# Attention values stored as high beside low: two products a step instead of three

## The chip, the cores and the metric

The kernel runs on one core of one Trainium2 chip, in one launch. The metric is the device time of a launch in microseconds (us). A core has a matrix engine (PE in the profile; PEld is its loading of the stationary operand), a vector engine (DVE), a scalar engine (ACT), a general engine (POOL), and a queue that issues transfers (SP). Each engine takes its own instructions strictly in the order in which they were written for it, and waits where an input or a buffer is not ready. Matrix products land in eight banks (PSUM) of 128 partitions by 512 float32 numbers; everything else lies in SBUF.

## The reference, cut to what matters

A small encoder: two layers on 512 tokens of width 1024, each of feed-forward block, token mixer, cross-attention into 256 memory tokens, and feed-forward block. The change is in the token mixer of the even layer, which runs once:

```python
def mixer_ab(h, w_in, w_out, q_gain, k_gain, sink, ang_2d, ang_1d):
    qa, ka, va, qb, kb, vb = jnp.split(h @ w_in, AB_SPLITS, axis=-1)
    ...
    out_a = global_gqa(qa, ka, va)              # 8 heads of 64, 2 key/value heads, all 512 keys
    ...
    out_b = window_gqa_sink(qb, kb, vb, sink)   # 8 heads of 64, keys within 128 tokens, a sink logit
    return jnp.concatenate([out_a, out_b], axis=-1) @ w_out
```

Each head computes softmax(q k) v. All is float32, and the kernel has to stay close to float32: it splits every operand z into a high part zh, rounded to the matrix engine's fast float32 form, and a low part zl = z - zh, and adds several products of the parts.

## The kernel before, in words

**Parts and products.** `split` (line 296) makes the parts of a tile with two instructions: ACT casts the source to the high part, DVE subtracts that from the source. `mm3` (line 307) then adds three products: high by high, high by low, low by high. A product of a stationary 128 by 128 tile and a moving tile of up to 512 columns is one MATMUL with one LDWEIGHTS.

**The even mixer** (`mixer_ab`, line 709) projects the tokens into queries, keys and values (lines 797 to 811), and then goes through 16 heads, numbered n: 0 to 7 are the dense A heads, 8 to 15 the windowed B heads. Two heads s = 0 and 1 make a pair that fills 128 rows of output, 64 each. The loop stands at lines 917 to 937. For each head it

- turns the softmax weights of this head (`turned`, line 857): for each block kk of 128 keys up to four PE transposes into a bank of kind "t", then a split into two parts in SBUF;
- computes the softmax weights of the head two further on (`weights_a`, line 819, or `weights_b`, line 834): scores on PE into banks of kind "a", a minimum over the keys on DVE, an exponential on ACT, a reciprocal on DVE, and a multiplication that POOL does for most blocks (`normalise`, line 648);
- multiplies the turned weights with the values (`attend`, line 867) into a bank of kind "d";
- does a piece of other work laid aside for this place: the last 512 columns of the projection (`last_columns`, A heads), or a quarter of a half of the output projection (`share`, B heads), both on PE into "d" banks as well.

An A head has 512 columns in each of four key blocks; a B head has 256, 384, 384 and 256, since a block of keys is seen by two or three blocks of queries.

**Values before.** `padded` (line 703) takes two slabs (SBUF tiles of 4 KB a partition, 27 in all), one for high and one for low, and clears them on POOL. In them a value head of 64 columns stands in a stationary tile of 128 columns beside 64 columns of zeros: on the left for s = 0, on the right for s = 1. So both heads of a pair add into one bank, each into its own 64 rows. `attend` calls `mm3`, three products for each key block, 24 for a pair. At the end of a pair the bank is split straight out of PSUM: one cast on ACT, one subtraction on DVE (lines 926 and 930).

**What sets the order.** All operations are first recorded (class `Graph`, line 64) with their tiles. `emit` (line 168) then goes through them with costs of its own for each instruction and writes each engine's instructions in the order in which they come ready by these costs, older ones first. Tiles of a kind are granted in the order in which they were asked for: 27 slabs, 14 smaller tiles "t2", 2 raw weight buffers, and banks "a" 3, "d" 2, "t" 3. A bank is granted anew when the last instruction that uses it has ended. So a change of a few instructions also moves others on every engine of this stage, since the planner places them anew.

**After the heads** the other half of the output projection follows (`down`, lines 938 to 940). Its weights come through the two raw buffers, of which one is held by the memory tokens until they are turned (`memory_tokens`, after head 13).

The odd layer's mixer (`mixer_c`, line 955) holds its values in another way: high and low side by side, two products for each block of weights, and at lines 1087 to 1092 a copy and an addition that bring the two halves together.

Of the kernel before, what the change touches and what calls it, by code (L numbers as in the profile page):

```python
# [12 lines left out]
F32 = mybir.dt.float32  # L13
F32R = mybir.dt.float32r
# [3 lines left out]
ALU = mybir.AluOpType  # L18
AX = mybir.AxisListType

P = 128
D = 1024
S = 512
NT = S // P
# [4 lines left out]
ROWS = S // GRID_W  # L29
# [223 lines left out]
class Kernel:  # L253
# [446 lines left out]
        )  # L700
        return sq[:, :w]

    def padded(self):
        tiles = [self.slab(F32R, (P, NT, 2, P)) for _ in range(2)]
        for z in tiles:
            self.nc.gpsimd.memset(z.bitcast(F32), 0.0)
        return tiles

    def mixer_ab(self, ln_i, last):
        nc, a = self.nc, self.a  # L710
        w_in, w_out = a["ab_w_in"], a["ab_w_out"]
# [3 lines left out]
        def halves():  # L715

            if not room:
                z = self.slab(F32, (P, 2, 512))
                room.extend([z[:, 0, :], z[:, 1, :]])
            return room.pop(0)  # L720
# [3 lines left out]
        for name, gain in (("q", "ab_q_gain"), ("k", "ab_k_gain"), ("b", None)):  # L724
            tab = halves()
            tab = tab.rearrange("p (t d) -> p t d", t=NT)
            src = a["rope_1d"] if gain is None else a["rope_2d"]
            for t in range(NT):
                nc.sync.dma_start(out=tab[:, t, :], in_=src.rearrange("(r c) d -> c r d", c=GRID_W)[16 * t : 16 * t + 16])
            if gain:  # L730
                gn = self.small(128, "gain", 1)
                nc.sync.dma_start(out=gn[:, 0:64], in_=a[gain][0:1, :].broadcast_to([P, 64]))
                for h in range(2):
                    nc.sync.dma_start(
                        out=gn[:, 64 + 32 * h : 96 + 32 * h],
# [18 lines left out]
            v = z.rearrange("p (pr s d) -> p s pr d", s=2, d=64)  # L754
            return v if s is None else v[:, s]

        def value(src, vp, t, n=1):

            dst = []
            for z in vp:  # L760
                v = z[:, t].rearrange("p v c -> p (v c)")
                dst.append(bass.AP(v.tensor, v.offset, [list(v.ap[0]), [256, n], [192, 2], [1, 64]]))
            self.split(src.rearrange("p (t v c) -> p t v c", t=n, v=2), *dst)

        def by_rows(z, natural):

# [19 lines left out]
        def keys(tile_, natural):  # L786

            got = []
            for s in range(2):
                ps = self.transposed([(t * P, P, tile_[:, t, s].rearrange("p c d -> p (c d)")) for t in range(NT)])  # L790
                both = self.pair()
                shape = lambda y: y.rearrange("p (r c) -> p r c", r=ROWS) if natural else y
                self.split(by_rows(ps, natural), *(shape(z) for z in both))
                got.append(both)
            return got

        w1, w0 = self.w_cols512(w_in, 512), self.w_cols512(w_in, 0)
        qa, qb, va = [halves() for _ in range(NT)], [halves() for _ in range(NT)], self.padded()
        ka, kb = (self.slab(F32, (P, NT, 2, 2, 64)) for _ in range(2))
        q = [self.pair()]  # L800
        for cg, t in ((1, 0), (1, 1), (1, 2), (0, 0), (1, 3), (0, 1), (0, 2), (0, 3)):
            ps = proj(self.ps("a"), t, w1 if cg else w0)
            if cg == 0:
                self.rope(self.rms(ps, 8), 8, tabs["q"], t, pairs(qa[t]))
                queries(qa, 0, False, q[0], [t])
                continue
            self.rope(self.rms(ps[:, 0:128], 2), 2, tabs["k"], t, ka[:, t])
            value(ps[:, 128:256], va, t)
            self.rope(ps[:, 256:512], 4, tabs["b"], t, pairs(qb[t], 0))
            if t == NT - 1:  # L810
                kA = keys(ka, False)
# [45 lines left out]
        def turned(p):  # L857

            got = []
            for kk in range(NT):  # L860
                ts = [t for t in range(NT) if (t, kk) in p]
                pt = self.transposed([(t * P, P, p[t, kk]) for t in ts])
                lo, hi = ts[0] * P, (ts[-1] + 1) * P
                got.append((lo, hi, [z[:, lo:hi] for z in self.split_t2(pt, lo, hi)]))
            return got

        def attend(po, s, pts, vp):
            for kk, (lo, hi, pt) in enumerate(pts):
                v = [z[:, kk, s, :] for z in vp]
                self.mm3(po[:, lo:hi], v, pt, s == 0 and kk == 0, s == 1 and kk == NT - 1, skip_group_check=True)  # L870

        w2 = self.w_cols512(w_in, 1024)
        vt, vt_, qb_ = self.t2(F32), [], {}
# [11 lines left out]
        def values_turned():  # L887
            ps = self.transposed([(t * P, P, vt[:, t * P : (t + 1) * P]) for t in range(NT)])
            vt_.append(self.t2(F32))
            nc.scalar.copy(vt_[0].rearrange("p (r c) -> p r c", r=ROWS), by_rows(ps, True))  # L890

        def values_b():
            value(self.transposed([(t * P, P, vt_[0][:, t * P : (t + 1) * P]) for t in range(NT)]), vb, 0, NT)

        def share(h, t):
            self.down_bank(acts[:4], [[z[:, b] for z in wa[h][b0]] for b0 in range(2) for b in range(2)], t, h, 1.0 / ALPHA)
# [4 lines left out]
        aside = {}  # L901
        for n in range(8):
            aside.setdefault((-1, -1, -1, 0, 1, 2, 3, 4)[n], []).append(lambda n=n: last_columns(n // 2, n % 2))
        vb, kB, wa, acts = [], [], {}, []
        aside.setdefault(2, []).append(lambda: vb.extend(self.padded()))
        aside.setdefault(5, []).append(lambda: (values_turned(), kB.extend(keys(kb, True))))
        aside[6] = [values_b]
        for n in range(8):
            h, t = divmod(n, 4)
            if t == 0:  # L910
                aside.setdefault(6 + 4 * h, []).append(lambda h=h: half_rows(h))
            aside.setdefault(8 + n, []).append(lambda h=h, t=t: share(h, t))
        heads = [(f, v, pr, s) for f, v in ((weights_a, va), (weights_b, vb)) for pr in range(4) for s in range(2)]
        us, po = [g(*at) for g, _, *at in heads[:2]], None
        for g in aside[-1]:
            g()
        for n, (f, v, pr, s) in enumerate(heads):
            pts = turned(us.pop(0))
            for g, _, *at in heads[n + 2 : n + 3]:
                us.append(g(*at))  # L920
            if s == 0:
                po = self.ps("d")
            attend(po, s, pts, v)
            if s == 1:
                if n < 8:
                    acts.append(self.split_t2(po))
                else:

                    h, l = self.pair()
                    self.split(  # L930
                        po.rearrange("p (r c) -> p c r", r=ROWS), *(z.rearrange("p (c r) -> p c r", r=ROWS) for z in (h, l))
                    )
                    acts.append((h, l))
            for g in aside.get(n, []):
                g()
            if n == 13:
                self.memory_tokens()
# [400 lines left out]
```

## Time and profile before

| | |
|---|---|
| time, median of 3 runs | 2215.97 us (2215.14 to 2216.75) |
| span of the profiled execution | 2218.7 us, 2.7 us above that median; no other time of this execution is given |
| PE busy | 2185.8 us, 99% of the span, 11264 products |
| PEld / DVE / ACT / POOL busy | 84% / 64% / 40% / 14% |
| the chain that ended last | PE 94%, DVE 3%, ACT 1%, POOL 1%, DMA 1%, issue 1% |
| mean granted PE clock | 0.996 |
| the even mixer in the span | from about 352 to about 584 us |

Shares are taken over the whole span, which strings together stages with different limits. A matrix product's own duration in the trace (382 ns on average) overlaps the next one's, so the pace is read from long stretches of products in the chain. "Idle before" is the time an engine stood still ahead of an instruction, with the one that released it. Nearly all instructions are recorded by a helper at line 143, so groups are told apart by the names of their tiles: "a", "d" and "t" are banks, but "t" is also the name that the "t2" tiles get, since numbers are left out.

### The profile page before, as it was taken

Reading aid. Unit: us, or ns where it says so; the run is one execution under the profiler, and the core shown is the slowest. Engines: PE = TensorE matmul, PEld = TensorE weight load, DVE = VectorE, ACT = ScalarE, POOL = GpSimd, SP = SyncE. Lnnn points to the kernel's source line nnn. Section 1 sums busy time; section 2 is a strip of 40 time slices with the busy share of each in tenths; the row PEclk is TensorE's granted clock in tenths of the full one; section 3 lists DMA queues with packets and bytes.
Section 4 is the critical chain, followed back from the end, with each engine's and each line's share of the span. In section 5 each row is a group of like instructions: output and inputs, shape, how many; then the busy total and the mean of one; then the engine's idle time right before and its main releaser. Section 6 shows DMA issues by size and latency. Waiting matters only on the chain.

```text
span 2218.7 us, 28479 instructions
## 1 busy us (share of the span) xinstructions
PE 2185.8 (99%) x11264; PEld 1863.8 (84%) x11264; DVE 1415.7 (64%) x2127; ACT 878.2 (40%) x1412; POOL 318.0 (14%) x431
## 2 busy tenths in 40 slices
PE   8999999999999999999999999999999999999998
PEld 7888888778998988888888888888989989888886
DVE  5566657788745756655765566567767557566556
ACT  4333333466443433333333233245554434333331
POOL 0000022544000000000300001214330000000002
PEclk9999999999999999999999999999999999999999
DMA  7443333102442642334334444235553325433342
GB/s 222 143 142 120 106 107 104 39 10 70 130 133 96 182 135 95 95 121 149 120 105 131 143 142 147 95 102 148 141 157 124 124 96 161 124 100 93 111 152 67
DMA packets 195221, 265.15 MB, mean 120 GB/s; under 512 B 8848, under 2 KB 139536, under 8 KB 195088
## 3 DMA queue, kind: packets, MB, share of 16 engines
q1 hardware_dynamic: 181136, 231.88, 32.9%
q0 software_dynamic: 13952, 31.46, 6.6%
q8 instruction: 88, 1.44, 0.3%
q14 instruction: 45, 0.37, 0.1%
HBM read 248.63 MB, written 4.19 MB: 114 GB/s over the span
## 4 chain that ended last, share of the span: by engine, by line
PE 94%; DVE 3%; ACT 1%; POOL 1%; DMA 1%; issue 1%; SPq 0%; DVEq 0%; POOLq 0%; ACTq 0%
PE a L143 59%; PE d L143 21%; PE t L143 14%; DVE slab L143 1%; DVE t L143 1%; ACT slab L143 1%; DVE x L143 0%; POOL slab L143 0%; DMA raw<-ab_w_out 0%; ACT t L143 0%; DMA slab<-t 0%; POOL rms8y L143 0%; ACT junk L143 0%; DMA x<-x 0%; POOL lny L143 0%
## 5 line engine op out<-in xcount | busy, mean ns | idle before, releaser
L143 PE MATMUL a<-xh,slab 128*128 128x512 f32 (+1 forms) x2960 | 892.9, 382 | 0.0
L143 PEld LDWEIGHTS a<-xh,slab 128*128 128x128 f32 x2960 | 549.1, 188 | 106.8
L143 PE MATMUL a<-xl,slab 128*128 128x512 f32 (+1 forms) x1480 | 565.1, 382 | 0.0
L143 PE MATMUL d<-slab,slab 128*128 128x512 f32 (+2 forms) x1856 | 448.8, 381 | 3.3 <-ACT slab L143 3.3
L143 DVE TENSOR_TENSOR slab<-raw,slab 128x1024 fp32r<-128x1024 f32 x300 | 368.8, 1250 | 92.7 <-ACT slab L143 92.2
L143 PEld LDWEIGHTS d<-slab,slab 128*128 128x128 f32 x1856 | 334.5, 188 | 67.3 <-ACT slab L143 5.1
L143 ACT CAST slab<-raw 128x1024 fp32r<-128x1024 f32 x300 | 304.3, 1048 | 206.2 <-DMA raw<-ffn_w_gate 176.4
L143 DVE TENSOR_TENSOR slab<-slab,slab 128x1024 fp32r<-128x1024 f32 (+2 forms) x220 | 254.0, 1177 | 177.8 <-ACT slab L143 104.7
L143 PEld LDWEIGHTS a<-xl,slab 128*128 128x128 f32 x1480 | 278.3, 188 | 53.4
L143 PE MATMUL a<-slab,slab 128*128 128x256 f32 (+3 forms) x1720 | 301.2, 321 | 3.7 <-DMA slab<-t 1.4
L143 PEld LDWEIGHTS a<-slab,slab 128*128 128x128 f32 x1720 | 250.0, 190 | 31.4 <-DVE slab L143 4.6
L143 ACT ACTIVATE t<-a 128x512 f32<-128x512 f32 (+3 forms) x105 | 58.1, 554 | 525.7 <-PE a L143 525.6
L143 ACT CAST slab<-slab 128x1024 fp32r<-128x1024 f32 (+1 forms) x180 | 174.3, 1000 | 135.6 <-DVE slab L143 135.5
L143 POOL DMA_DIRECT2D slab<-ffn_w_down x40 | 48.6, 1255 | 1008.7 <-DMA slab<-ffn_w_down 639.6
L143 PE MATMUL t<-slab,slab 128*128 128x512 f32 (+1 forms) x792 | 185.4, 380 | 0.0
L143 PEld LDWEIGHTS t<-slab,slab 128*128 128x128 f32 x792 | 142.9, 188 | 29.8
L143 DVE TENSOR_TENSOR slab<-a,t 128x512 f32<-128x512 f32 x72 | 49.8, 692 | 175.7 <-PE a L143 175.7
L143 DVE TENSOR_TENSOR slab<-t,slab 128x512 fp32r<-128x512 f32 (+2 forms) x213 | 133.1, 649 | 40.0 <-ACT slab L143 39.5
L143 ACT CAST slab<-t 128x512 fp32r<-128x512 f32 (+2 forms) x213 | 114.6, 565 | 100.9 <-PE t L143 61.8
L143 DVE SCALAR_TENSOR_TENSOR x<-d,x 128x512 f32<-128x512 f32 x168 | 114.9, 686 | 47.4 <-PE d L143 46.9
L143 POOL TENSOR_TENSOR t<-t,l 128x256 f32<-128x256 f32 (+2 forms) x104 | 84.2, 831 | 344.1 <-DVE l L143 343.8
L143 PE MATMUL a<-slab,xh 128*128 128x256 f32 (+1 forms) x432 | 101.2, 328 | 2.2 <-ACT slab L143 1.6
(104 smaller groups left out, 1912.5 us busy)
## 6 DMA issues: line engine op xcount, KB each, us to landing
slab<-ffn_w_down SPq DMA_DIRECT2D x100, 512.0 KB
raw<-ffn_w_gate SPq DMA_DIRECT2D x40, 1024.0 KB
raw<-ffn_w_up SPq DMA_DIRECT2D x40, 1024.0 KB
slab<-ffn_w_down POOLq DMA_DIRECT2D x40, 512.0 KB, 9.7
slab<-t SPq DMA_DIRECT2D x96, 128.0 KB
raw<-mem_w_kv SPq DMA_DIRECT2D x8, 1024.0 KB
raw<-mem_w_kv SPq DMA_DIRECT2D x16, 512.0 KB
raw<-mem_w_q SPq DMA_DIRECT2D x8, 1024.0 KB
```

Of the source, the lines that this page charges most:

```text
L143: op.call = lambda: fn(*args, **kw)
```

## The change

The values now have one slab. A value head's 64 high columns stand beside its 64 low columns in one stationary tile of 128 columns; there are no zeros, and `padded` with its POOL memsets is gone. `value` splits into the two halves of that slab.

`attend` takes a bank for each head instead of one for a pair. For each key block it issues two products, the value tile with the high and with the low part of the weights. Rows 0 to 63 of the bank then hold the high values' sum, rows 64 to 127 the low values'. (The product of low by low, which was left out before, is now included.) ACT copies rows 64 to 127 into the head's 64 rows of a "t2" tile `o`, and DVE adds rows 0 to 63 to it. When the pair is complete, `o` is split by `split_pair`, now with SBUF as its source.

```diff
-        def value(src, vp, t, n=1):
-
-            dst = []
-            for z in vp:
-                v = z[:, t].rearrange("p v c -> p (v c)")
-                dst.append(bass.AP(v.tensor, v.offset, [list(v.ap[0]), [256, n], [192, 2], [1, 64]]))
-            self.split(src.rearrange("p (t v c) -> p t v c", t=n, v=2), *dst)
+        def value(src, v, t, n=1):
+
+            v = v[:, t : t + n]
+            self.split(src.rearrange("p (t s c) -> p t s c", t=n, s=2), v[:, :, :, 0], v[:, :, :, 1])
...
-        qa, qb, va = [halves() for _ in range(NT)], [halves() for _ in range(NT)], self.padded()
+        qa, qb, va = [halves() for _ in range(NT)], [halves() for _ in range(NT)], self.slab(F32R, (P, NT, 2, 2, 64))
...
-        def attend(po, s, pts, vp):
+        def attend(o, s, pts, v, natural):
+
+            po = self.ps("d")
             for kk, (lo, hi, pt) in enumerate(pts):
-                v = [z[:, kk, s, :] for z in vp]
-                self.mm3(po[:, lo:hi], v, pt, s == 0 and kk == 0, s == 1 and kk == NT - 1, skip_group_check=True)
-
-
+                for i, z in enumerate(pt):
+                    nc.tensor.matmul(
+                        po[:, lo:hi], v[:, kk, s].rearrange("p z c -> p (z c)"), z,
+                        start=kk == 0 and i == 0, stop=kk == NT - 1 and i == 1, skip_group_check=True,
+                    )
+            shape = lambda z: z.rearrange("p (r c) -> p c r", r=ROWS) if natural else z
+            y = o[64 * s : 64 * s + 64]
+            y = y.rearrange("p (c r) -> p c r", r=ROWS) if natural else y
+            nc.scalar.copy(y, shape(po[64:128]))
+            nc.vector.tensor_tensor(out=y, in0=shape(po[0:64]), in1=y, op=ALU.add)
...
-        aside.setdefault(2, []).append(lambda: vb.extend(self.padded()))
+        aside.setdefault(2, []).append(lambda: vb.append(self.slab(F32R, (P, NT, 2, 2, 64))))
...
             if s == 0:
-                po = self.ps("d")
-            attend(po, s, pts, v)
+                o = self.t2(F32)
+            attend(o, s, pts, v[0], n >= 8)
             if s == 1:
-                if n < 8:
-                    acts.append(self.split_t2(po))
-                else:
-
-                    h, l = self.pair()
-                    self.split(
-                        po.rearrange("p (r c) -> p c r", r=ROWS), *(z.rearrange("p (c r) -> p c r", r=ROWS) for z in (h, l))
-                    )
-                    acts.append((h, l))
+                acts.append(self.split_pair(o))
```

More of the change, by code (lines that the diff above doesn't have):

```diff
@@ L701, in rms @@
         return sq[:, :w]
[L703 to L707, printed above, removed]
     def mixer_ab(self, ln_i, last):
@@ L892, in values_b @@
         def values_b():
-            value(self.transposed([(t * P, P, vt_[0][:, t * P : (t + 1) * P]) for t in range(NT)]), vb, 0, NT)
+            value(self.transposed([(t * P, P, vt_[0][:, t * P : (t + 1) * P]) for t in range(NT)]), vb[0], 0, NT)
         def share(h, t):
@@ L912, in mixer_ab @@
             aside.setdefault(8 + n, []).append(lambda h=h, t=t: share(h, t))
-        heads = [(f, v, pr, s) for f, v in ((weights_a, va), (weights_b, vb)) for pr in range(4) for s in range(2)]
-        us, po = [g(*at) for g, _, *at in heads[:2]], None
+        heads = [(f, v, pr, s) for f, v in ((weights_a, [va]), (weights_b, vb)) for pr in range(4) for s in range(2)]
+        us, o = [g(*at) for g, _, *at in heads[:2]], None
         for g in aside[-1]:
```

## The prediction

> **What bounds the kernel now.** I read the page's head first, then the chain of waits, then busy time by stretches of the even mixer, then its groups by shape, and last the order of time where two engines come close.
>
> ```profile
> span 2218.7 us, 28479 instructions
> PE 94%; DVE 3%; ACT 1%; POOL 1%; DMA 1%; issue 1%; SPq 0%; DVEq 0%; POOLq 0%; ACTq 0%
> ```
>
> Over the whole span PE is the bound: the chain that ended last is 94% PE. So a product taken away is worth its full pace, as long as its stage is PE's too. That has to be read from the stage, the even mixer:
>
> ```profile
> core 0: us, PE busy (x) PEld busy (x) DVE busy (x) ACT busy (x) POOL busy (x), PEclk, DMA share, GB/s
> 430.90:449.95 19.05, 18.89 (x101) 15.66 (x100) 15.45 (x40) 12.22 (x31) 12.37 (x15) 1.00 0.00 1
> 449.95:468.98 19.03, 18.86 (x102) 15.68 (x100) 14.80 (x35) 11.98 (x28) 7.48 (x9) 1.00 0.01 1
> 468.98:489.37 20.39, 18.79 (x108) 15.45 (x107) 17.07 (x38) 15.39 (x34) 9.26 (x13) 1.00 0.00 1
> 489.37:510.07 20.70, 18.14 (x110) 14.80 (x110) 16.94 (x45) 14.79 (x35) 8.47 (x23) 1.00 0.23 51
> 510.07:519.70 9.63, 9.63 (x57) 8.22 (x56) 7.80 (x30) 7.75 (x22) 6.04 (x12) 1.00 0.01 3
> 519.70:534.48 14.78, 14.70 (x91) 12.56 (x89) 13.81 (x37) 8.95 (x27) 6.25 (x15) 1.00 0.36 109
> 534.48:549.36 14.88, 14.63 (x91) 12.79 (x89) 11.73 (x40) 9.91 (x30) 7.69 (x14) 1.00 0.24 57
> 430.90:549.36 118.46, 113.64 (x647) 95.15 (x646) 97.60 (x262) 81.00 (x203) 57.55 (x96) 1.00 0.12 30
> ```
>
> Each of the first seven rows is about a pair of heads; together they are heads 0 to 13, and the last row is their sum. PE is busy 113.64 of 118.46 us, but DVE 97.60, far above its 64% of the whole span. In the third and fourth rows PE already stands still for 1.6 and 2.6 us. Here DVE is the engine to watch.
>
> **What is removed.** An A head has 4 x 512 columns, a B head 256 + 384 + 384 + 256, and each key block loses one product of three. The stationary tile is 128 columns wide before and after, so the pace stays.
>
> ```profile
> 880.49 42.84 PE a L143 x189
> ...
> 1112.48 2.88 PE d L143 x24
> ```
>
> 189 products of 512 columns take 42.84 us on the chain, 0.227 us each; 24 of 256 columns in the feed-forward block take 2.88, 0.120 each; 384 columns lie half way, 0.173 (an estimate). A heads: 8 x 4 x 0.227 = 7.25 us. B heads: 8 x (2 x 0.173 + 2 x 0.120) = 4.69. PE loses 11.9 us, of which 10.8 in heads 0 to 13 and 1.2 in heads 14 and 15. That is the ceiling.
>
> **What is added.** The odd mixer already holds its values so, and shows the new instructions; the last two rows are the split that is moved, and POOL's memsets.
>
> ```profile
> L143 ACT COPY t<-d 64x512 f32<-64x512 f32 x14 | 8.2, 583 | 1.3 <-PE d L143 1.0
> L143 DVE TENSOR_TENSOR t<-d,t 64x512 f32<-64x512 f32 x12 | 8.2, 680 | 1.0 <-ACT t L143 0.8
> ...
> L143 DVE TENSOR_TENSOR slab<-d,slab 128x512 fp32r<-128x512 f32 x8 | 5.5, 691 | 1.9 <-ACT slab L143 1.9
> L143 POOL MEMSET slab<- 128x1024 f32 x4 | 3.8, 957 | 0.0
> ```
>
> Half the partitions don't make them cheaper: 680 ns for 64 rows, 691 for 128. So 16 copies put 9.3 us on ACT, and 16 additions 10.9 us on DVE. The eight splits stay, with the same counts and sizes. ACT has room: 81.0 + 14 x 0.583 = 89.2 of 118.46 - 10.8 = 107.7 us. DVE has none: 97.6 + 14 x 0.680 = 107.1 us. To give PE's whole saving, DVE would have to be busy 99.5% of the stretch.
>
> **Heads 0 to 5 (three rows, 58.5 us).** DVE cannot reach 99.5%, since some of its waits are built in:
>
> ```profile
> 435.68 1.41 DVE L143 SCALAR_TENSOR_TENSOR slab<-t,slab 64x512 fp32r<-64x512 f32 x2 [0.60 <-ACT slab L143]
> 448.12 0.69 DVE L143 TENSOR_TENSOR slab<-d,slab 128x512 fp32r<-128x512 f32 x1 [0.27 <-ACT slab L143]
> 451.26 1.89 DVE L143 TENSOR_TENSOR slab<-t,slab 128x512 fp32r<-128x512 f32 x3 [2.30 <-ACT slab L143]
> ```
>
> The 2.30 us before the first turned bank of a pair is slack that an addition can fill. The 0.60 before a pair's queries is not: ACT's two casts stand directly ahead of it. Take DVE's work of about 15.1 us a pair (first two rows), add 1.36, the 0.60, and 0.24 for the contention below: 17.3. PE would allow 19.04 - 1.81 = 17.2. So a pair goes from 19.04 to about 17.3: -1.7 each for the first two. The third row has 17.07 + 1.36 + 0.60 + 0.24 = 19.3 against 20.39: -1.1. Sum -4.5; ends -5.4 (all of PE's) and +4.1 (3 x 1.36, if no gap can be filled).
>
> **Heads 6 and 7 (20.70 us).** Here the chain runs through DVE, ACT and POOL, and PE waits for them. Two additions come in (+1.4) and eight products less stand in the way (at most -1.8). I take 0, between -1.8 and +2.6 (both additions and both ACT copies, 2.5, in the chain).
>
> **Heads 8 to 13 (39.3 us).** A pair saves 1.17 us of PE and costs 1.36 of DVE. In the three rows DVE has 33.34; with 4.08, 3 x 0.60 and 3 x 0.24 it is 39.9, against 39.29 now. So PE's saving is worth nothing here: +0.6; ends -3.5 (all of PE's) and +4.1.
>
> **Contention with POOL.** The moved split's subtraction now reads both inputs from SBUF; before, one came from PSUM.
>
> ```profile
> 526.86 3.72 POOL L143 TENSOR_TENSOR t<-t,l 128x256 f32<-128x256 f32 x4 [5.02 <-DVE l L143]
> ...
> 522.35 1.21 DVE L143 TENSOR_TENSOR slab<-raw,slab 128x1024 fp32r<-128x1024 f32 x1
> 528.34 1.77 DVE L143 TENSOR_TENSOR slab<-raw,slab 128x1024 fp32r<-128x1024 f32 x1
> ...
> 1517.58 1.15 DVE L143 TENSOR_TENSOR slab<-t,slab 128x512 fp32r<-128x512 f32 x1 [0.23 <-ACT slab L143]
> 1562.34 0.68 DVE L143 TENSOR_TENSOR slab<-t,slab 128x512 fp32r<-128x512 f32 x1
> ```
>
> A weight split with both inputs in SBUF takes 1.21 us, and 1.77 while POOL multiplies; the odd mixer's 512-wide subtractions take 0.68, and one 1.15. So the eight cost between 0 and 0.47 each more; I take the half, 0.24, since POOL is busy 57.55 of 118.46 us. [...]
>
> **The end (from 549.36).** Heads 14 and 15 save 1.17 us of PE, but the last weights arrive late:
>
> ```profile
> 552.71 7.30 DMA raw<-ab_w_out
> 560.11 1.33 ACT slab L143 x2
> 561.48 1.79 PE d L143 x8
> ```
>
> Their transfer starts when the memory tokens are turned, and PE needs them 8.8 us later whatever it does between. So the saving becomes waiting: 0. The last pair's parts come one copy and one addition (1.26 us) later; products of the other three pairs stand ready as cover. I take +0.3, between -1.2 and +1.3.
>
> **The start (352 to 430.9).** Two memsets (1.9 us) fall on an idle POOL. A slab less lets weight splits stand earlier in DVE's order, one of them ahead of the RMS multiplication of the queries.
>
> ```profile
> 398.21 0.47 PE L143 MATMUL t<-ident,slab 128*128 128x128 f32 x1 [2.02 <-POOL slab L143]
> 398.68 4.59 PE a L143 x14
> 396.00:398.00 2.00, 0.18 (x1) 0.00 (x0) 2.00 (x2) 0.00 (x0) 2.00 (x1) 1.00 0.00 0
> 398.00:400.00 2.00, 1.79 (x5) 1.50 (x6) 1.81 (x3) 0.54 (x2) 1.83 (x3) 0.53 0.00 0
> ```
>
> After a stall of 2.02 us the granted clock falls to 0.53, and the 14 products after it take 4.59 us instead of 3.17. The new order puts one product more before that stall, so it is 0.2 shorter: -0.3 with small shifts; ends -1.7 (the slow clock goes too) and +1.2 (the split holds up the queries). [...]
>
> The transfers on SP's queue stand in the same order as before; POOL's queue loses the memsets and keeps the rest but for neighbours changing places.
>
> **The sum.** -4.5 + 0 + 0.6 + 0.3 - 0.3 = -3.9 us: a span of 2214.8 instead of 2218.7. The profiled span stands 2.7 us above the median of the runs, 2215.97; the same difference gives 2212.1 us.
>
> **The rivals.**
> 1. *PE's whole saving.* DVE's order packs, and turned banks and minima are never late: -9 to -12 us, some 2205.5. For it: PE is 99% busy over the span. Against it: the 99.5% of DVE.
> 2. *The bank comes free too late (slower).* There are two "d" banks, and each head now takes one; it is free when DVE's addition ends, and that stands among the minima of the scores. Before, a pair's bank was free at 448.12 + 0.69 and PE wanted it for the next pair only after the turned banks, split from 451.26 on. If the addition comes x late, PE waits x for each of 16 heads, and the change loses from x = 11.9 / 16 = 0.75 us, little more than one minimum (677 ns) ahead of it. At x = 1.1: 17.6 - 11.9 = +5.7, 2221.7. Against it: the odd mixer lives with two such banks at 17.75 of 22.40 us of DVE.
> [...]
>
> ```profile
> L143 POOL TENSOR_TENSOR t<-t,l 128x512 f32<-128x512 f32 x24 | 25.3, 1083 | 31.6 <-DVE l L143 31.6
> L143 DVE TENSOR_REDUCE mn<-a 128x1 f32<-128x512 f32 x32 | 21.1, 677 | 0.6 <-PE a L143 0.2
> ```
>
> That the change does not do what it says is no rival: the built order has two products for each key block.
>
> **How the numbers follow.** The forecast, DVE taking about two thirds of the saving, has 0.58 (2209 to 2215); rival 1 has 0.18, rival 2 0.14, rival 3 0.10. The bound for faster and slower is 0.2%, 4.4 us, which is about what a measurement tells from no change. Faster: rival 1 and some two fifths of the forecast's cases, 0.41. Slower: rival 2 mostly, and a little of rival 3, 0.13. The same: 0.46. The range leaves out the far side of rivals 1 and 2: 2205.5 to 2219.5.
>
> **What would show it.** Products fall by 64. DVE from 430.9 on is busy 93% or more, its wait of 2.3 us before a pair's turned banks is gone, and PE has new waits on DVE "slab". The first pairs come every 17.3 us, and heads 8 to 13 still take 39 to 40. Wrong would be: PE without waits in heads 6 to 13; products that wait for a "d" bank; subtractions of 1.2 us or more, always beside POOL; a changed stage after 584 us.

## The result, and the profile after

The changed kernel takes 2224.54 us (median; 2222.21 to 2225.27), the kernel before, run beside it, 2216.75. The ratio is 1.003, with a 95% interval of 1.002 to 1.004: it is slower by 7.8 us, where 3.9 us less was forecast, and it lies outside the range. The profiled execution took 2225.27 us. The two profiled spans differ by less than the times, 4.8 us (2218.7 and 2223.5): behind the mixer, where the program is the same, the profile of the kernel before is 2.9 us longer, and over the 14 profiles of this document that part takes 1620.9 to 1624.7 us. So a profile shows the mixer, and the times show the kernel.

The head of the page of the changed kernel, and its share of the chain that ended last:

```profile
span 2223.5 us, 28346 instructions
PE 2183.6 (98%) x11200; PEld 1856.1 (83%) x11200; DVE 1427.0 (64%) x2143; ACT 886.1 (40%) x1428; POOL 317.0 (14%) x427
...
PE 93%; DVE 3%; ACT 2%; POOL 1%; issue 1%; DMA 0%; SPq 0%; DVEq 0%; POOLq 0%; ACTq 0%
```

The products went as they should, 11200 instead of 11264. Over the whole span nothing looks amiss. So the stage has to be read again. The next two views are busy time by stretches, of the changed kernel and then, from head 4 on, of the one before (its first two rows stand in the prediction). Each stretch begins with the first turned bank of heads 0, 2, 4, 6, 8, 10 and 12, and the last ends with that of head 14. (Two banks of transposes under the same names turn the B heads' values, one ahead of head 6 and one ahead of head 8; they are not counted as heads' banks.) The numbers behind the window are its length, busy time of the engines (with instructions), granted PE clock, and DMA.

```profile
core 0: us, PE busy (x) PEld busy (x) DVE busy (x) ACT busy (x) POOL busy (x), PEclk, DMA share, GB/s
432.36:450.97 18.61, 18.07 (x93) 13.70 (x92) 15.53 (x39) 12.57 (x31) 8.98 (x11) 1.00 0.00 1
450.97:469.01 18.04, 17.50 (x94) 14.03 (x93) 16.23 (x38) 12.86 (x31) 7.97 (x9) 1.00 0.01 1
469.01:485.38 16.37, 16.12 (x93) 12.96 (x92) 14.87 (x35) 13.60 (x30) 7.85 (x12) 1.00 0.00 1
485.38:508.50 23.12, 16.16 (x73) 12.99 (x72) 19.24 (x41) 12.91 (x31) 9.07 (x17) 0.73 0.18 43
508.50:525.30 16.80, 15.63 (x82) 12.20 (x82) 12.83 (x42) 13.83 (x35) 7.79 (x16) 0.96 0.02 4
525.30:539.79 14.49, 13.47 (x76) 10.65 (x75) 12.78 (x31) 8.50 (x24) 8.14 (x16) 1.00 0.14 38
539.79:561.85 22.06, 19.92 (x109) 16.30 (x108) 18.59 (x58) 15.67 (x42) 10.85 (x17) 0.92 0.44 120
```

```profile
468.98:487.41 18.43, 17.63 (x102) 14.66 (x100) 15.11 (x36) 13.43 (x31) 7.30 (x13) 1.00 0.01 1
487.41:503.05 15.64, 13.69 (x81) 10.99 (x82) 14.32 (x35) 11.28 (x25) 7.68 (x17) 1.00 0.31 67
503.05:519.54 16.49, 15.08 (x89) 12.67 (x88) 12.37 (x44) 13.06 (x36) 8.62 (x19) 1.00 0.01 2
519.54:534.32 14.78, 14.70 (x90) 12.56 (x88) 13.65 (x37) 8.95 (x25) 6.25 (x15) 1.00 0.34 106
534.32:552.12 17.80, 17.55 (x111) 15.40 (x110) 14.25 (x44) 11.64 (x34) 8.63 (x15) 1.00 0.32 85
```

Up to head 6 the change gains: the three stretches take 18.61, 18.04 and 16.37 us instead of 19.05, 19.03 and 18.43. Then it loses 7.5 us in heads 6 and 7 and 4.3 in heads 12 and 13, with +0.3 and -0.3 in the two pairs between. In the two stretches that lose, the granted clock (the column ahead of the DMA share) is 0.73 and 0.92, and the 0.96 between is the end of the first of them; in the kernel before it is 1.00 in all of these stretches. This column is the finding. Nothing in the forecast's stages had it. Heads 12 and 13 also hold other work now: the mixer's end after them, with 13 products less, is 2.1 us shorter (39.88 instead of 41.98), where the change itself takes 8 away.

What PE does there. First its rows in order of time, of the changed kernel (start, busy time, and in brackets the idle time ahead and what ended it), then the same times in windows that run from one clock change to the next:

```profile
485.38 0.60 PE L143 MATMUL t<-ident,t 128*128 128x128 f32 x4
488.66 0.66 PE L143 MATMUL t<-ident,t 128*128 128x128 f32 x4 [2.68 <-DVE slab L143]
...
504.60 1.12 PE L143 MATMUL t<-ident,t 128*128 128x128 f32 x4 [3.15 <-DVE slab L143]
505.37 2.91 PE L143 MATMUL d<-slab,slab 128*128 128x512 f32 x6
...
542.78 0.39 PE L143 MATMUL d<-slab,slab 128*128 128x256 f32 x1 [1.29 <-DVE t L143]
543.56 1.44 PE L143 MATMUL d<-slab,slab 128*128 128x512 f32 x3 [0.40 <-DVE x L143]
```

```profile
485.81:489.22 3.41, 0.73 (x6) 0.42 (x4) 2.62 (x7) 3.41 (x10) 2.81 (x3) 1.00 0.00 0
489.22:492.64 3.42, 2.89 (x11) 2.29 (x11) 2.79 (x5) 1.31 (x3) 0.95 (x5) 0.50 0.00 0
492.64:496.05 3.41, 3.41 (x11) 2.75 (x11) 2.02 (x4) 1.77 (x3) 0.01 (x1) 0.50 0.02 5
...
499.46:502.88 3.42, 1.39 (x7) 0.61 (x5) 3.25 (x7) 2.41 (x7) 3.15 (x3) 1.00 0.00 0
502.88:506.29 3.41, 1.69 (x6) 1.58 (x7) 3.26 (x6) 0.54 (x2) 0.74 (x4) 0.50 0.58 147
506.29:509.70 3.41, 3.41 (x12) 2.77 (x11) 2.32 (x8) 1.08 (x5) 0.61 (x1) 0.50 0.73 161
...
540.42:543.84 3.42, 1.73 (x12) 1.29 (x11) 3.36 (x14) 3.37 (x11) 1.58 (x4) 1.00 1.05 273
543.84:547.25 3.41, 3.41 (x12) 2.63 (x12) 2.55 (x5) 1.42 (x4) 2.02 (x4) 0.50 0.55 113
```

Three times PE stands still, twice for 2.7 and 3.2 us, once in several waits close together. Each time the granted clock falls to 0.50, for 3.41 or 6.83 us: from 489.22 on, from 502.88 on, while the second stall still lasts, and from 543.84 on. Six products of 512 columns then take 2.91 us, and from the first's start to the next product it is 0.45 us for each, instead of 0.227. The second stall has its cause in DVE's order (first the changed kernel, then the one before):

```profile
500.54 3.40 DVE L143 TENSOR_TENSOR slab<-raw,slab 128x1024 fp32r<-128x1024 f32 x2
503.87 1.87 DVE L143 TENSOR_TENSOR slab<-t,slab 128x512 fp32r<-128x512 f32 x3
```

```profile
496.90 1.39 DVE L143 TENSOR_TENSOR slab<-raw,slab 128x1024 fp32r<-128x1024 f32 x1
498.21 0.21 DVE L143 RECIPROCAL l<-l 128x1 f32<-128x1 f32 x2
498.44 1.89 DVE L143 TENSOR_TENSOR slab<-t,slab 128x512 fp32r<-128x512 f32 x3
```

The two subtractions that split the output weights (in `half_rows`) stood 10 us apart before, at 486.99 and 496.90. Now they stand side by side, directly ahead of head 7's turned banks. For 3.4 us no "t" bank comes free, and PE has nothing else ready.

For the whole mixer the length can be taken apart. It is counted here from the last of DVE's additions `x<-t,x` ahead of it (328.24 us before, so it holds the last 24 us of the feed-forward block too) to the start of the last instruction of its last normalisation (594.10). "Still" is the length less PE's busy time. "Slow clock" is PE's busy time in windows of 1 us, times what the granted clock lacks to 1. "Rest" is the other busy time.

| | mixer | still | slow clock | rest |
|---|---|---|---|---|
| before | 265.86 | 9.56 | 1.65 | 254.65 |
| after | 273.32 | 18.04 | 9.10 | 246.18 |
| difference | +7.46 | +8.48 | +7.45 | -8.47 |

In this account what the products save is spent on standing still, and the slow clock is the loss. It is an account, not yet a cause: with the clock held, other waits might have been longer.

### The profile page after: what moved, and what is told of

The parts are those of the page before. It is cut to its first block, busy times and chain, and to the rows that moved or that the text cites. A ratio compares the mean times of both kernels' runs of the same rounds, so it can differ in the third digit from the quotient of the medians.

```text
span 2223.5 us, 28346 instructions
## 1 busy us (share of the span) xinstructions
PE 2183.6 (98%) x11200; PEld 1856.1 (83%) x11200; DVE 1427.0 (64%) x2143; ACT 886.1 (40%) x1428; POOL 317.0 (14%) x427
## 4 chain that ended last, share of the span: by engine, by line
PE 93%; DVE 3%; ACT 2%; POOL 1%; issue 1%; DMA 0%; SPq 0%; DVEq 0%; POOLq 0%; ACTq 0%
PE a L143 58%; PE d L143 21%; PE t L143 14%; DVE slab L143 1%; DVE t L143 1%; ACT t L143 1%; ACT slab L143 1%; POOL slab L143 0%; DVE x L143 0%; DMA x<-x 0%; DVE mn L143 0%; ACT junk L143 0%; POOL lny L143 0%; POOL t L143 0%; POOL rms8y L143 0%
## 5 line engine op out<-in xcount | busy, mean ns | idle before, releaser
L143 PEld LDWEIGHTS d<-slab,slab 128*128 128x128 f32 x1792 | 326.7, 190 | 68.8 <-ACT slab L143 3.9
L143 DVE TENSOR_TENSOR slab<-t,slab 128x512 fp32r<-128x512 f32 (+2 forms) x221 | 139.8, 658 | 37.8 <-ACT slab L143 37.6
L143 ACT CAST slab<-t 128x512 fp32r<-128x512 f32 (+2 forms) x221 | 119.3, 567 | 103.6 <-PE t L143 64.9
```

Of the source, the lines that this page charges most:

```text
L143: op.call = lambda: fn(*args, **kw)
```

## The experiments

Two theories were on trial. **DVE load**: the 16 additions fill DVE, and whatever order it works in, they cost what the products save. **Order and clock**: the additions and the missing products shift the planner's order; a few stalls come out at about 2 us or longer (the one of 2.02 us in the kernel before had a slow clock after it), and that clock makes the loss. All ratios are to the kernel before, with 95% intervals; "mixer" and its parts are from each run's profiled execution.

| | time, ratio | mixer | still | slow clock | rest |
|---|---|---|---|---|---|
| e1 filler in heads 5 to 8 | 1.0014 (1.0005 to 1.0023) | 267.14 | 14.50 | 1.71 | 250.93 |
| e2 filler in all heads | 1.0035 (1.0022 to 1.0048) | 274.08 | 14.40 | 1.70 | 257.98 |
| e3 no additions | 0.9985 (0.9976 to 0.9994) | 260.74 | 14.70 | 1.39 | 244.65 |
| e4 splits later | 0.9992 (0.9983 to 1.0001) | 265.17 | 14.64 | 4.88 | 245.65 |
| e5 only A heads | 1.0019 (1.0009 to 1.0029) | 268.32 | 15.68 | 3.41 | 249.23 |
| e6 only B heads | 0.9998 (0.9989 to 1.0008) | 265.16 | 11.84 | 1.71 | 251.61 |
| e7 e4, split on POOL | 0.9985 (0.9976 to 0.9995) | 262.98 | 14.46 | 1.66 | 246.86 |
| e8 e4, banks first | 0.9985 (0.9975 to 0.9994) | 262.69 | 13.33 | 1.51 | 247.85 |
| e9 e8, slab held | 0.9972 (0.9962 to 0.9983) | 259.97 | 11.78 | 0.00 | 248.19 |
| e10 e8, split on POOL | 0.9977 (0.9968 to 0.9986) | 261.27 | 13.07 | 0.00 | 248.20 |
| e11 e9 and e10 | 0.9963 (0.9950 to 0.9975) | 259.09 | 11.56 | 0.00 | 247.53 |
| e12 before, ranks of e8 | 1.0008 (0.9999 to 1.0017) | 267.28 | 10.81 | 1.71 | 254.76 |

**e1: more work for PE in heads 5 to 8.** In `attend`, ahead of the real products:

```diff
+            if 5 <= n <= 8:
+                for kk, (lo, hi, pt) in enumerate(pts):
+                    nc.tensor.matmul(
+                        po[:, lo:hi], v[:, kk, s].rearrange("p z c -> p (z c)"), pt[0],
+                        start=kk == 0, stop=kk == NT - 1, skip_group_check=True,
+                    )
```

> Heads 5 to 8 get their products with the high part once more, ahead of the real ones and into the same bank; the first real product starts the bank anew, so that the result stays. PE gets 12 products of 512 columns and 4 of 256 or 384 more, 12 x 0.227 + 0.7 = 3.4 us; DVE, ACT and the two weight splits side by side stay as in the changed kernel (2224.5 us; before 2216.8). Theory clock: of the changed kernel's loss, 7.4 us is half clock after three stalls of 2 us and more. The added products fill stalls that PE would spend waiting, which fall under 2 us, and the clock stays: 2218 to 2221, faster than the changed kernel by 3 to 6 us although PE has more to do. Theory DVE load: the DVE chain sets the time, fillers change nothing: 2224.5. Theory PE: fillers come on top: 2228.

2221.51 us, 3.0 us above before instead of 7.8, though PE has 3.4 us more to do. (That is half a microsecond above the clock theory's range; the kernel before took 1.7 us more beside this run than beside the first. The intervals of the two ratios, 1.0005 to 1.0023 here and 1.002 to 1.004, just meet.) PE's row at the first stall, and the window behind it:

```profile
486.99 0.66 PE L143 MATMUL t<-ident,t 128*128 128x128 f32 x4 [1.69 <-DVE slab L143]
```

```profile
488.00:490.00 2.00, 1.87 (x15) 1.49 (x14) 1.83 (x4) 1.10 (x3) 0.42 (x3) 1.00 0.00 0
```

The stall of 2.68 is 1.69 us, that of 3.15 became two of 1.02 and 0.68 (both ended by ACT), and the clock stays at 1.00 (one slow stretch is left, at 537.9). In the table slow clock falls by 7.4 us and standing still by 3.5, against 4.8 more of the rest. One thing is not as expected: the planner set DVE's two weight splits a little apart again (494.97 and 497.60), so the relief at the second stall is not the filler's alone. At the first, ACT and DVE work in the same order as in the changed kernel but for one copy and one addition that moved a few places, so there it is the filler's in the main. That work added to PE makes the kernel faster can't be had from a theory in which DVE's load alone sets the time. It is what the clock theory says, with a share of the new order that this run does not separate.

**e2: the filler in all heads.** The same lines with the condition `n >= 0`: PE's products as many as before, with the additions and copies.

> The same filler in all 16 heads: PE's work is that of the kernel before (64 products of 11.9 us put back), DVE and ACT keep the additions and copies, and the weight splits stand apart again in DVE's order. So it shows what additions and copies cost beside an unchanged PE. Theory DVE load: DVE's 10.9 us and ACT's 9.3 us don't fit; as slow as the changed kernel or slower: 2224 to 2228. Theory clock and order: no stall of 2 us in heads 0 to 13, granted clock 1.00 from 431 us on: 2217 to 2220.

2226.24 us: here the DVE theory holds. No stall of 2 us is left after the start, one stretch of 3.41 us is slow, and yet the mixer takes 8.2 us more than before. The additions and copies are far from free beside an unchanged PE: 4.8 us of it is standing still. The other 3.3 stand in the "rest" with as many products; what they are these rows don't show (in the kernel before a product's row lasts 382 ns on average, where products of 512 columns come 227 ns apart, so short waits may hide in the rows).

**e3: no additions.**

```diff
             nc.scalar.copy(y, shape(po[64:128]))
-            nc.vector.tensor_tensor(out=y, in0=shape(po[0:64]), in1=y, op=ALU.add)
```

> The 16 additions on VectorE are left out (the low half of each head's product is dropped from the output), the ACT copies stay. The weight splits stand apart again in DVE's order. Theory DVE load: without 10.9 us on DVE the products' saving shows: 2205 to 2209. Theory order alone (additions are cheap, the splits side by side do the harm): about the same, 2206 to 2210, but then the run that only moves the splits gains too. If stalls of 2 us and half clock remain without the additions, both fall: 2215 or more.

This kernel leaves the low half of each product out of the result; it is there for its time alone. 2215.11 us, mixer 5.1 us shorter than before: a gain, but under half of the 11.9 us of products. A stall of 3.06 us at head 6's banks (484 to 487) stands here too, with a slow stretch from 486.41 on. So neither side had it whole. Against the changed kernel the mixer is 12.6 us shorter, of which 7.7 is slow clock: and the weight splits stand apart again (482.87 and 496.40), so the 4.9 us left are not the additions' alone. Against e4 and e9 below, which keep them, it is 4.4 us shorter and 0.8 longer, so what they cost hangs on the order; and even without them PE cannot collect its saving.

**e4: the weight splits later.** The order alone:

```diff
         def half_rows(h):
+            at = len(nc.ops)
             wa[h] = [self.w_rows_pairs(w_out, 128 * b, 512 * h) for b in range(2)]
+            for op in nc.ops[at:]:
+                if not op.dma:
+                    op.rank += 100
```

> The changed kernel, with the splits of the output weights ranked 100 places later in the planner, so that they no longer stand side by side ahead of head 7's turned banks; nothing else is changed. Theory order: the stall of 3.15 us at 501 to 504 and the half clock after it go (3.15 + about 2.7), also part of the third stall at 540 to 544: 2216 to 2219. Theory DVE load: the same amount of DVE work brings a stall of 2 us or more elsewhere, the clock falls there: 2222 to 2226.

2216.72 us, 1.8 us below before, with an interval that just takes in 1; the mixer is 8.2 us shorter than the changed kernel's, with the same instructions. Half of that is slow clock (9.10 to 4.88), most of the other half standing still (18.04 to 14.64). The stall of 3.15 us is gone. This is the largest step with the same work, and it is one of order: the order theory had 2216 to 2219, the DVE theory 2222 to 2226. The first stall stays, though, with 6.83 us at a granted clock of 0.50 after it, from 488.73 on:

```profile
488.19 0.66 PE L143 MATMUL t<-ident,t 128*128 128x128 f32 x4 [2.67 <-DVE slab L143]
```

**e5 and e6: one kind of head alone.** `attend`, the values' layout and the split of the output as before in heads 8 to 15 (e5) or in heads 0 to 7 (e6).

> Heads 0 to 7 as in the changed kernel, heads 8 to 15 as before: PE loses 7.25 us, DVE gains 8 additions, 5.4 us; the weight splits stand side by side ahead of head 7's banks as in the changed kernel. Theory order and clock: stalls of 2.7 and 3.1 us and half clock as in the changed kernel; mixer 7 to 11 us longer than before's 265.9. Theory DVE load as predicted (the first three pairs gain 4.5 us, the rest nothing): 3 to 5 us shorter.

> Heads 8 to 15 as in the changed kernel, heads 0 to 7 and the order around the weight splits as before: PE loses 4.7 us, DVE gains 5.4. Theory order and clock: no stall of 2 us, mixer 1 to 4 us shorter than 265.9, since the last pairs gain (2.9 us in four of the runs so far). Theory DVE load as predicted: heads 8 to 13 give nothing, +0.6 and +0.3: 266 to 267.

Only A heads: slower by 0.19%, with stalls of 2.68 and 2.79 us (ended at 487.55 and 502.46) as in the changed kernel, but each with one slow stretch of 3.41 us instead of 6.83, and a mixer 2.5 us longer, not 7 to 11. Only B heads: no difference that can be told, mixer 0.7 us shorter, below the 1 to 4 expected: waits of 1.30 and 0.40 us in heads 12 and 13 (534.38, 535.16) brought a slow stretch there, from 536.24 on. Neither mixer lies in a range of either theory. The two parts make +1.8 us in the mixer, both together +7.5. The table says where the difference lies: standing still adds up (6.1 and 2.3 us, 8.5 together), the rest does too (-5.4 and -3.0, -8.5 together), and the slow clock does not (1.8 and 0.1, 7.5 together). Stalls as long as the changed kernel's brought half as much slow clock in e5; the last section comes back to this.

**e7: the moved split's subtraction on POOL** (on top of e4).

```diff
-                acts.append(self.split_pair(o))
+                hi, lo = self.pair()
+                nc.scalar.copy(hi, o)
+                nc.gpsimd.tensor_tensor(out=lo, in0=o, in1=hi.bitcast(F32), op=ALU.subtract)
+                acts.append((hi, lo))
```

> As the kernel with the splits 100 places later (mixer 265.2, 2216.7), but the subtraction that splits each pair's output into high and low part goes to GpSimd: DVE loses 8 x 0.7 to 0.9 = 5.6 to 7 us, GpSimd gains about 8 x 1.1. Theory DVE load: mixer 3 to 6 us shorter still, 260 to 262. Theory order: DVE's sum is not what bounds it, only which instruction stands ahead of which; 264 to 267.

2214.64 us, mixer 2.2 us shorter than e4's, between the two theories' ranges, and 3.2 of slow clock less: without the slow clock it is 1.0 us longer. The weight splits moved too (from 505.78 and 511.83 to 489.16 and 503.53), so this run does not tell load from order.

**e8: head 6's turned banks first** (on top of e4).

```diff
+            at = len(nc.ops)
             pts = turned(us.pop(0))
+            if n == 6:
+                for op in nc.ops[at:]:
+                    op.rank -= 120
```

> As the kernel with the splits 100 places later, but head 6's turned banks are ranked 120 places earlier, so that ACT casts the first of them ahead of head 7's last two exponentials. Theory: the stall of 2.7 us at 486 to 488 and its half clock (3.4 us of PE) come from casts and subtractions that stand behind other work; mixer 3 to 6 us shorter, 259 to 262. Rival: the exponentials it displaces make the next stall, of the same size: 264 to 267.

2214.94 us, with a mixer of 262.69 us, less of a gain than the 259 to 262 expected. What the edit does is seen in ACT's rows, and on PE in the wait of the same transposes:

```profile
484.75 0.69 ACT L143 ACTIVATE t<-a,mn 128x512 f32<-128x512 f32 x1
485.34 0.19 ACT L143 ACTIVATION_READ_ACCUMULATOR t<-a,mn 128x1 f32 x1
485.43 0.57 ACT L143 CAST slab<-t 128x512 fp32r<-128x512 f32 x1
485.90 0.70 ACT L143 ACTIVATE t<-a,mn 128x512 f32<-128x512 f32 x1
```

```profile
486.78 0.66 PE L143 MATMUL t<-ident,t 128*128 128x128 f32 x4 [0.22 <-DVE slab L143]
```

One cast goes ahead of head 7's last two exponentials, and the stall of 2.67 us is 0.22. In the changed kernel all the exponentials stood ahead of the casts, which began at 487.29. The same held in the kernel before, with the casts at 487.23; but there PE came to head 6's banks 2.0 us later and waited less, 0.58 us at the second of them and 0.81 at the first product:

```profile
487.41 0.66 PE L143 MATMUL t<-ident,t 128*128 128x128 f32 x4 [0.58 <-ACT t L143]
```

That it is the missing third products that bring PE there early fits e1, whose fillers shorten this wait; no run tests it alone. The mixer's gain over e4, 2.5 us, is less than the slow clock that went (3.4). The 3.2 us after the stall went with it; 1.7 more is the stretch at the keys, which e8 lacks after the same wait (2.59 us in e4, 2.58 here); and one of 1.5 us came new, at 504.54. Standing still fell by 1.3 us only, and the rest grew by 2.2: other waits came in the stall's place.

**e9: the slab that was given up is held** (on top of e8). Nothing uses it:

```diff
+        hold = [self.slab()]
+        nc.gpsimd.memset(hold[0].bitcast(F32), 0.0)
...
+            if n == 7:
+                nc.gpsimd.tensor_copy(self.small(1, "mn"), hold.pop()[:, :1].bitcast(F32))
```

> As the kernel with splits later and head 6's banks first (mixer 262.7, of which the first pair's queries come 108.8 us after the mixer's start, before 106.5 to 107.4), and a second slab, written with zeros once on GpSimd, is held from the start to head 7, as the values' zero padding held it before. Nothing else reads it. Theory slab: the one slab less is what reordered the start (the projection weights' splits stand earlier, ahead of instructions that PE waits for), so with it held the first queries come at 106.5 to 107.5 again and the mixer takes 260 to 261. Rival: the start is longer for another reason (the values' new layout); 108.5 to 110 and 262.5 as now.

2212.82 us, mixer 2.7 us shorter, of which 1.5 is the slow stretch that e8 has at 504.54. PE's first transposes of the keys, in the changed kernel, in e8 and in e9:

```profile
399.46 0.33 PE L143 MATMUL t<-ident,slab 128*128 128x128 f32 x1 [2.57 <-POOL slab L143]
```

```profile
400.07 0.33 PE L143 MATMUL t<-ident,slab 128*128 128x128 f32 x1 [2.58 <-POOL slab L143]
```

```profile
397.97 0.33 PE L143 MATMUL t<-ident,slab 128*128 128x128 f32 x1 [2.02 <-POOL slab L143]
```

With the slab held the wait is that of before, 2.02 us, and the first pair's queries come 106.4 us after the mixer's start, where e8 had 108.8, neither with slow clock on the way, and before 107.4, with 1.65 us of it. One slab of 27 less in use, in itself a gain, made the way to those queries 2.4 us longer, by what the planner did with it: in the changed kernel and in e8 a weight split stands ahead of the RMS multiplication of the queries (392.09 and 394.87 in the changed kernel), in e9 as before it doesn't.

**e10 and e11: POOL again, and all together.** e10 is e8 with e7's edit, e11 is e9 with it.

> Splits later and head 6's banks first, with the subtraction of each pair's output split on GpSimd. Theory DVE load: what DVE sheds (8 x 0.7 to 0.9 us) comes on top of 262.7: 259.5 to 261.5. Theory order: with the 2.7 us stall already gone, DVE's sum no longer sets anything but the pace of a few pairs: 262 to 263.5.

> All of it together: splits later, head 6's banks first, the slab held, the subtraction on GpSimd. If the parts add: 258 to 260 in the mixer, 2211 to 2213 of time where before takes 2218.6. If one of them is no real gain: 260.5 to 262.

e10: 2213.72 us, mixer 261.27. That lies in the DVE theory's range, but e8's 262.69 had a slow stretch and this run has none: less the slow clock it is 0.1 us off e8. On top of e9 the same edit gives 0.9 us in the mixer, and in the times 1.2 us over e8 and 2.9 over e9, with intervals that overlap. So the 5.6 to 7 us that DVE sheds come back by half at the most: its sum alone is not the bound. The edit is not a clean test of that either, since the planner again moved the weight splits (503.87 and 507.55 in e8, 489.84 and 502.15 in e10). e11: 2209.95 us, 0.9963 (0.9950 to 0.9975) of before: 8.8 us faster than the kernel before beside it, by the change that lost 7.8 and four edits that take no product away. In its stretches of heads 6 to 9 the clock stays at 1.00:

```profile
480.38:495.86 15.48, 13.00 (x77) 9.65 (x75) 14.52 (x36) 14.24 (x33) 9.22 (x17) 1.00 0.16 35
495.86:512.65 16.79, 15.56 (x85) 11.99 (x84) 14.68 (x48) 13.18 (x36) 9.91 (x19) 1.00 0.12 32
```

Each of the steps from e4 to e11 has an interval that overlaps its neighbour's; what is clear of the noise is the way from the changed kernel to e4, and from e4 to e11.

**e12: the ranks alone.** The kernel before with the edits of e4 and e8.

> The kernel before, three products per key block and no additions, with the same two changes of rank alone. If the gain of the later runs is the products' and not the order's, the mixer stays at 265 to 267. If the order alone brings it, 262 to 263.

2220.23 us, 0.08% above before, mixer 1.4 us longer. So these two edits of rank are no gain by themselves: what the later runs gain needs the missing products. That no other order would make the kernel before faster this run does not show; none was sought for it.

## Why the prediction was wrong

By its own steps, mixer stages against the forecast:

- **Where the heads lie.** Several of the forecast's rows do not end where the heads do. The transposes at 485.36 of the kernel before turn the B heads' values (ACT copies that bank at 486.77), and head 6 begins at 487.41. Its row for heads 6 and 7, 489.37 to 510.07 and 20.70 us, stands for 487.41 to 503.05, 15.64 us; heads 8 to 13 take 49.07 us, not 39.3. By the forecast's own rule the true stretches of heads 8 to 13 would have given 40.27 us of DVE's work + 4.08 + 1.8 + 0.72 = 46.9 of 49.07, so -2.2 instead of +0.6 (an estimate).
- **What is removed** (-11.9 us): 64 products fell, as said. PE's busy time without the slow clock fell by 8.5 only; e2 shows a difference of the same size (3.3) with no product less.
- **What is added**: copies 582 ns and additions 683 ns each, sums 9.3 and 10.9 us, as said.
- **Heads 0 to 5** (-4.5): 56.51 us became 53.02, -3.49. The sum is 1 us off, but not by the forecast's parts: the first two pairs gained 0.44 and 0.99 us instead of 1.7 each, the third 2.06 instead of 1.1. The 17.3 us a pair were not reached (18.61, 18.04), nor 93% of DVE: it is busy 83% and 90% of these stretches. With the start's order mended e9 has 17.7 and 17.8. That the sum came this near is luck in part.
- **Heads 6 and 7: "I take 0, between -1.8 and +2.6"**: +7.48. **Heads 8 to 13: "+0.6; ends -3.5 and +4.1"**: +4.28 (49.07 us became 53.35), all of it in heads 12 and 13. These two are the steps that failed, the first above all. They compared sums of busy time by stage. The stalls came from which instruction stands ahead of which: two weight splits of 1.6 to 1.9 us, side by side, and casts behind exponentials, with fewer products in front of PE. The bounds held additions in the chain, but not that the planner, given other times, moves other work: 8.2 us of e4's mixer against the changed one's hang on that alone.
- **The clock.** The prediction had the row: after a stall of 2.02 us at the start 14 products took 4.59 us instead of 3.17, 1.4 more. It put this price into no bound of heads 6 to 13, where a slow clock came three times: +7.45 us, as much as the whole loss. Taken off both mixers it leaves 264.22 us, against 264.21 for the kernel before. And e4's, without the slow clock, is 3.9 us below before's, the same figure as the forecast's sum. That is a coincidence: e4 has another order, and by stages the forecast's terms were off by up to 7 us.
- **The end** (+0.3): from the first turned bank of head 14 to the end of the mixer 41.98 us became 39.88, -2.1; e6, in which the A heads are as before, has the same. About 1 us of this is work that moved into heads 12 and 13 (13 products less, not 8; an estimate at 0.2 us each). "The saving becomes waiting" was wrong: PE stands still for 0.04 us in this stretch.
- **The start** (-0.3): +1.3 up to the first turned bank. That a slab less puts a weight split ahead of the RMS multiplication of the queries was right; the stall at the keys became 0.55 us longer, not 0.2 shorter, and a second wait on POOL takes 1.53 us (ended at 413.39), where the longest such wait before, behind the first, took 0.75.
- **Contention** (0.24 each): the 41 subtractions of 512 columns took 682 ns each, now 49 take 721, so the eight new ones about 0.92 us instead of 0.69: 0.23 each, as forecast. It is a mean of two kinds: four of the eight took 1.09 to 1.47 us, each beside a POOL multiplication, and the other four 0.68 to 0.69, three of them beside one too (512.52, 526.70 and 559.80). So POOL beside it did not always make a subtraction longer.

The rows of that last point, before and then after:

```profile
L143 DVE TENSOR_TENSOR slab<-t,slab 128x512 fp32r<-128x512 f32 x41 | 26.2, 682 | 8.1 <-ACT slab L143 8.1
```

```profile
L143 DVE TENSOR_TENSOR slab<-t,slab 128x512 fp32r<-128x512 f32 x49 | 33.5, 721 | 6.9 <-ACT slab L143 6.8
```

Of the rivals, the whole saving did not come. That each of the eight subtractions waits out a POOL multiplication of 1083 ns, which had a chance of 0.10 as rival 3, no run shows: the longest of them took 1.47 us, 0.78 more than the shortest. The late "d" bank came once for more than half a microsecond, in the row at 542.78 with its 1.29 us: it is part of the third slow stretch, and a small part of the loss.

## What to carry to other kernels

Where several engines pass work round in a ring, less work for the bound engine takes cover from the others (here PE came to head 6's banks 2.0 us earlier and stood still there for 2.68 us, where it had waited 0.58 and 0.81): before costing the gain, look for what the others have queued in one piece, and how long the bound engine can go on without it. Price a PE stall like those here (2.02 to 3.15 us, or 1.29 and 0.40 close together) at its length and the clock that may fall after it, in these runs 1.4 to 1.7 us for each slow stretch of 3.41. And where a planner sets the order, a change of times is a change of order everywhere in its stage; read the new order before the sums, and try moving one block by rank before giving the change up.

## What the hardware did that was not expected

The slow stretches were taken from the trace's clock record in all 14 profiles. Within the mixers there are none of another length than 3.41 or 6.83 us, all at a granted clock of 0.50, and in each execution all begin on one grid of 3.413 us (in the changed kernel at 400.48, 489.22, 502.88 and 543.84, which are 26, 4 and 12 steps apart), whose place differs from one execution to the next (the kernel before has its one at 398.14, 2.34 us ahead of the changed kernel's first). So the same stall can cost or not. The changed kernel waits 2.57 us at the keys, e8 2.58; the windows of that grid, first of the changed kernel, then of e8:

```profile
397.06:400.48 3.42, 1.02 (x5) 0.89 (x6) 1.29 (x3) 0.62 (x3) 3.24 (x3) 1.00 0.18 14
400.48:403.89 3.41, 3.41 (x10) 2.60 (x9) 3.33 (x11) 1.23 (x2) 1.63 (x2) 0.50 0.54 140
```

```profile
395.31:398.73 3.42, 2.19 (x13) 1.55 (x11) 3.21 (x6) 1.22 (x2) 1.22 (x2) 1.00 0.00 0
398.73:402.14 3.41, 2.06 (x10) 1.72 (x11) 1.21 (x6) 1.64 (x4) 2.19 (x3) 1.00 0.50 100
```

In the one the stall falls into one window, PE is busy 30% of it, and the next window has half the clock. In the other it is shared by two windows, 64% and 60% busy, and the clock stays. Over all 14 mixers, from 345 to 600 us, every window of the grid at full clock in which PE was busy less than 43% was followed by a slow one (9 windows, 20 to 43% busy), none over 56%; between, 7 of 19 were (those were 45 to 56% busy). These bounds are read off the same 14 profiles and were tried on no other kernel.

One consequence for the table above: a single slow stretch in or out, 1.4 to 1.7 us there, can be chance in one profiled execution. The steps from e8 to e10 and of e6 are no larger than that in the mixer, so there the times over several executions count. It may also be why e5's two stalls, of 2.68 and 2.79 us, cost one slow stretch each where the changed kernel's cost two; no run shows this apart from the order.
